# A fixed TensorE order for the first attention, with PSUM banks of its own, in a two-layer diffusion backbone

## The chip, the cores and the metric

The kernel runs on one core of one Trainium2 chip. The metric is the device time of one launch in microseconds (us). A core has a matrix engine (TensorE, PE in the profile), a vector engine (VectorE, DVE), a scalar engine (ScalarE, ACT), GpSimd (POOL) and SyncE (SP), which issues the transfers. Each works through its own instruction list in order, and they wait for each other on counters (semaphores). TensorE writes its results into PSUM, eight banks of 512 fp32 columns on 128 partitions; DVE and ACT read them there.

## The reference

Two DeepNorm layers over 1024 latent tokens and 256 context tokens, width 1024, 16 heads of 64. The change concerns the mixer of the first layer only: windowed attention with a sink, rotary embeddings and a SiLU gate.

```python
def mixer_a(u, uc, w_in, w_out, sink, rope, ctx_out):
    q, k, v, g = _split_a(u @ w_in)          # 16 query heads, 4 key/value heads
    ...                                      # rotary embedding on q and k
    def block(bi):                           # blocks of 128 tokens
        ...
        mask = (jnp.abs(qi[:, None] - kj[None, :]) <= A_WINDOW) & (kj >= 0)[None, :] & (kj < S)[None, :]
        s_lat = jnp.einsum('bqkgd,bjkd->bkgqj', qb, kb).astype(jnp.float32) * scale
        s_lat = jnp.where(mask, s_lat, NEG_INF)
        s_ctx = jnp.einsum('bqkgd,bckd->bkgqc', qb, kc).astype(jnp.float32) * scale
        p = jax.nn.softmax(jnp.concatenate([s_lat, s_ctx, s_sink], axis=-1), axis=-1)
        o = jnp.einsum('bkgqj,bjkd->bqkgd', p_lat, vb) + jnp.einsum('bkgqc,bckd->bqkgd', p_ctx, vc)
    ...
    y = (o * jax.nn.silu(g)) @ w_out
    ...                                      # context tokens attend to the context alone
```

The second layer has a neighbourhood attention in this place; its code is not changed.

## The kernel before

The first attention (attention A) works on eight pairs of heads p; within a pair on ten blocks of 128 tokens b (blocks 8 and 9 are the context), within a block on the two heads h. One (p, b, h) is a *sub*, number k from 0 to 159; the two subs of a block are a *unit*. A sub sees four key tiles of 128 (b = 0 and 7), five (b = 1 to 6) or two (b = 8 and 9). Pair p has subs 20p to 20p + 19.

The steps of a sub k, by engine:
- scores S(k), in `qkA` on TensorE: the query in two halves of precision (l = 0 and 1) against the keys, four matmuls into one tile of two PSUM banks (`S_A`)
- `sm_first`: mask and minimum on DVE (L318), exp on ACT (L325); `sm_second`: reciprocal on DVE (L329), product on POOL (L330)
- transposes T(k), in `sm_transpose` on TensorE (L337): one per key tile, into another tile of two banks (`T_A`); then ACT copies them rounded (the cast, L341, `pth_A`), and DVE subtracts that copy from them (L343, `ptl_A`): the probabilities as a high and a low part. Both parts hold a whole unit and have two buffers
- values of a unit, in `pvA_fn` on TensorE (L734): first with the high part, then with the low part, into one bank for two blocks (`pvA`); behind every odd block the two halves of this bank are added into `otmp` (copy on ACT L743, add on DVE L744) and multiplied by the gate on POOL (L747). After block 9 a pair's result is written out (L751)

PSUM is one pool for the whole kernel: the tag "big" has two slots of two banks, which scores and transposes take in turn, and the tag "one" has four slots of one bank for projections and values.

`att_steps` writes the order of the pieces: row k holds T(k), S(k + 3) and half a unit's values, the high part two rows after the unit's second sub and the low part one row later. `merge` mixes into a pair's rows the projections that fill TensorE, those of the gate of pair p and of the queries of pair p + 1: pieces of 8 × 3 matmuls for each of three chunks (512, 512 and 256 tokens), three matmuls to a piece (L208 to L210: high weight by high and low token parts, low weight by high part). It takes the next fill piece while fill is behind its even share of the cost. The instructions then go to a list scheduler, which sets each engine's order by priorities (`lift`) and readiness, so the built order is not quite the order of the code.

## Time and profile before

| | |
|---|---|
| time, median of 3 runs | 1444.14 us (1442.26 to 1444.5) |
| profiled execution | 1443.36 us, its span 1441.6 us |
| PE busy | 1392.6 us, 97% |
| DVE, ACT, POOL busy | 987.3, 733.6, 630.8 us |
| first attention, first scores to the end of pair 6 | about 98 to 544 us |

The span is the time from the first to the last instruction of the core. The prediction shows the rows it uses of four views: the busy line, windows by stage, the waits of an engine and the timeline. In the timeline a row is the start, the duration, the engine, the line, the operation, output and inputs by their names in the program (numbers left out) and the count of like instructions. A matmul's duration includes its way through the array, so the cost of one on a busy TensorE is the distance to the start of the next.

### The profile page before, as it was taken

Reading aid. Unit: us, or ns where it says so; the run is one execution under the profiler, and the core shown is the slowest. Engines: PE = TensorE matmul, PEld = TensorE weight load, DVE = VectorE, ACT = ScalarE, POOL = GpSimd, SP = SyncE. Lnnn points to the kernel's source line nnn. Section 1 sums busy time; section 2 is a strip of 40 time slices with the busy share of each in tenths; the row PEclk is TensorE's granted clock in tenths of the full one; section 3 lists DMA queues with packets and bytes.
Section 4 is the critical chain, followed back from the end, with each engine's and each line's share of the span. In section 5 each row is a group of like instructions: output and inputs, shape, how many; then the busy total and the mean of one; then the engine's idle time right before and its main releaser. Section 6 shows DMA issues by size and latency. Waiting matters only on the chain. (4 is left out here: it accounts for less than half of the span.)

```text
span 1441.6 us, 25151 instructions
## 1 busy us (share of the span) xinstructions
PE 1392.6 (97%) x8816; PEld 1215.4 (84%) x8816; DVE 987.3 (68%) x2216; ACT 733.6 (51%) x1561; POOL 630.8 (44%) x779
## 2 busy tenths in 40 slices
PE   9999999999999999999999999999999999998995
PEld 5887888888888888788898899888988899887775
DVE  4658888878888789566433765555565565667698
ACT  4336776677676778333222545544454444557310
POOL 0326766666666657233211333333233323336664
PEclk9999999999999999999999999999999999999998
DMA  9472114123122114433287565564555565384353
GB/s 367 171 234 81 53 59 132 46 78 97 66 78 63 56 61 128 128 132 132 74 256 217 160 192 159 140 166 145 170 150 156 144 179 146 103 208 145 115 133 93
DMA packets 117229, 195.05 MB, mean 135 GB/s; under 512 B 9328, under 2 KB 57840, under 8 KB 117104
## 3 DMA queue, kind: packets, MB, share of 16 engines
q1 hardware_dynamic: 117104, 193.45, 44.5%
q8 instruction: 70, 1.15, 0.3%
q14 instruction: 55, 0.45, 0.1%
HBM read 141.51 MB, written 51.90 MB: 134 GB/s over the span
## 5 line engine op out<-in xcount | busy, mean ns | idle before, releaser
L330 POOL TENSOR_SCALAR s_B<-s_B,rs_B 128x640 f32<-128x640 f32 (+1 forms) x128 | 101.9, 797 | 292.0 <-DVE rs_B L329 250.9
L208 PE MATMUL pj<-uBh,wh 128*128 128x512 f32 (+1 forms) x448 | 175.9, 393 | 0.0
L209 PE MATMUL pj<-uBl,wh 128*128 128x512 f32 (+1 forms) x448 | 170.2, 380 | 0.0
L210 PE MATMUL pj<-uBh,wl 128*128 128x512 f32 (+1 forms) x448 | 170.0, 379 | 0.0
L325 ACT ACTIVATE s_B<-s_B,m_B 128x640 f32<-128x640 f32 (+1 forms) x128 | 102.9, 804 | 127.9 <-DVE m_B L318 127.7
L325 ACT ACTIVATE s_A<-s_A,m_A 128x641 f32<-128x641 f32 (+2 forms) x160 | 119.5, 747 | 88.5 <-DVE m_A L318 73.5
L164 POOL TENSOR_TENSOR wl<-wr,wh 128x512 fp32r<-128x512 f32 x64 | 87.7, 1371 | 157.8 <-ACT wh L162 135.4
L330 POOL TENSOR_SCALAR s_A<-s_A,rs_A 128x640 f32<-128x640 f32 (+2 forms) x160 | 127.1, 794 | 58.5 <-DVE rs_A L329 56.3
L318 DVE CUSTOM_DVE_ANT_0 s_A<-S_A,msk,nsk 128x640 f32<-128x640 f32 (+2 forms) x160 | 123.6, 774 | 34.0 <-PE S_A L706 17.7
L343 DVE TENSOR_TENSOR pt_B<-T_B,pt_B 128x640 fp32r<-128x640 f32 (+1 forms) x128 | 101.0, 789 | 63.4 <-ACT pt_B L341 62.9
L208 PE MATMUL pj<-uAh,wh 128*128 128x512 f32 (+1 forms) x384 | 139.9, 364 | 0.0
L209 PE MATMUL pj<-uAl,wh 128*128 128x512 f32 (+1 forms) x384 | 137.6, 358 | 0.0
L210 PE MATMUL pj<-uAh,wl 128*128 128x512 f32 (+1 forms) x384 | 137.3, 357 | 0.0
L343 DVE TENSOR_TENSOR ptl_A<-T_A,pth_A 128x640 fp32r<-128x640 f32 (+2 forms) x160 | 114.0, 713 | 15.3 <-PE pvA L734 7.1
L337 PE MATMUL T_A<-ident,s_A 128*128 128x128 f32 x672 | 101.0, 275 | 12.1 <-DVE m_A L318 8.6
L337 PEld LDWEIGHTS T_A<-ident,s_A 128*128 128x128 f32 x672 | 77.2, 140 | 40.2 <-issue 16.6
L341 ACT CAST pt_B<-T_B 128x640 fp32r<-128x640 f32 (+1 forms) x128 | 84.4, 659 | 47.8 <-PE T_B L337 47.4
L318 DVE CUSTOM_DVE_ANT_0 s_B<-S_B,bias 128x640 f32<-128x640 f32 (+1 forms) x128 | 100.5, 785 | 10.6 <-PE S_B L1037 9.6
L341 ACT CAST pth_A<-T_A 128x640 fp32r<-128x640 f32 (+2 forms) x160 | 96.5, 603 | 16.7 <-PE T_A L337 14.0
L210 PEld LDWEIGHTS pj<-uBh,wl 128*128 128x128 f32 x448 | 84.3, 188 | 16.7
L337 PE MATMUL T_B<-ident,s_B 128*128 128x128 f32 x608 | 88.3, 274 | 6.0 <-POOL gB L1078 2.3
L209 PEld LDWEIGHTS pj<-uBl,wh 128*128 128x128 f32 x448 | 84.7, 189 | 9.1
(219 smaller groups left out, 3885.3 us busy)
## 6 DMA issues: line engine op xcount, KB each, us to landing
kB<-kdB SPq DMA_DIRECT2D x64, 320.0 KB, 5.3
gw<-in_wadaT SPq DMA_DIRECT2D x48, 256.0 KB, 2.8
vdB<-st SPq DMA_DIRECT2D x20, 512.0 KB, 3.4
vB<-vdB SPq DMA_DIRECT2D x16, 640.0 KB, 4.8
wada<-in_wadaC SPq DMA_DIRECT2D x16, 512.0 KB, 9.7
kdB<-st SPq DMA_DIRECT2D x16, 512.0 KB, 2.9
qdB<-st SPq DMA_DIRECT2D x16, 512.0 KB, 3.5
qB<-qdB SPq DMA_DIRECT2D x32, 256.0 KB, 4.6
```

The source lines that it names most:

```text
L164: e.tensor_tensor(lo, r, f32(hi), ALU.subtract)
L208: mm(pt[:, :n], hi[:, sl], rh, start=kt == 0, stop=False)
L209: mm(pt[:, :n], hi[:, sl], rl, start=False, stop=False)
L210: mm(pt[:, :n], lo[:, sl], rh, start=False, stop=kt == KT - 1)
L318: nc.vector.tensor_tensor_reduce(outp, sc, in1, scale, init if init is not None else 3e38, ALU.add, ALU.min, accum_out=s.m)
L325: nc.scalar.activation(s.t[:, :n], s.t[:, :n], AF.Exp, bias=s.m, scale=-1.0, accum_out=s.sum)
L330: nc.gpsimd.tensor_scalar(s.t[:, : s.w], s.t[:, : s.w], s.rs, 1.0, ALU.mult, ALU.mult)
L337: nc.tensor.transpose(tp[:, k * P : (k + 1) * P], s.t[:, src * P : (src + 1) * P], ident)
L341: nc.scalar.copy(pt.hi[:, :n, hl, :], tv)
L343: nc.vector.tensor_tensor(pt.lo[:, :n, hl, :], tv, f32(pt.hi[:, :n, hl, :]), ALU.subtract)
```

## The change

Five things, all of attention A:
- PSUM is opened anew for each stage. In attention A it holds one tile of three banks for all transposes (`T_A`, allocated once: h = 0 uses its left end, h = 1 its right end, where five tiles meet in the middle bank, which is transposed last), one slot of two banks for scores, two slots for projections and one for values. Behind the first block of the output stage it is opened again with the old slots.
- For pairs 0 to 6 all matmuls and transposes are pinned: TensorE keeps the order of the code.
- `merge` takes fill at an even rate, and at most one fill piece with 512 columns between two steps.
- An even block's values go both halves together, in the row where the low half stood; odd blocks stay. In pairs 2, 4 and 6 the first three S pieces stand one step later.
- The copies of a value bank both come before the adds, at a priority of 60.

```diff
--- before.py
+++ after.py
@@ -34,6 +34,7 @@
 
 AHEAD_A, LIFT_A = 3, 80
 AHEAD_B, LIFT_B = 3, 40
+LIFT_PV = 60
 BARE_B = 108
 
 GATED_LAST = 1 << 20
@@ -82,7 +83,16 @@
 
 def build(tc, i, out):
     nc = tc.nc
-    mm = nc.tensor.matmul
+    pinned = []
+
+    def pin(ins):
+
+        if pinned:
+            tc.keep_in_program_order(ins)
+
+    def mm(*a, **kw):
+        pin(nc.tensor.matmul(*a, **kw))
+
     dma = nc.sync.dma_start
     es = ExitStack()
 
@@ -92,13 +102,29 @@
         return p, st
 
     dr = es.enter_context(tc.tile_pool(name="dr", bufs=1, space=DRAM))
-    ps = es.enter_context(tc.tile_pool(name="ps", bufs=1, space=PSUM))
-
-    def psbig(name):
-        return ps.tile([P, 1024], F32, tag="big", bufs=2, name=name)
-
-    def psone(name):
-        return ps.tile([P, 512], F32, tag="one", bufs=4, name=name)
+
+    class Banks:
+
+
+        def open(self, name, att=False):
+            self.st = ExitStack()
+            self.ps = self.st.enter_context(tc.tile_pool(name=name, bufs=1, space=PSUM, reuse_waits="tile"))
+            self.att = att
+            if att:
+
+                self.t3 = self.ps.tile([P, 1536], F32, tag="t3", bufs=1, name="T_A")
+
+        def big(self, name):
+            return self.ps.tile([P, 1024], F32, tag="big", bufs=1 if self.att else 2, name=name)
+
+        def one(self, name):
+            if self.att:
+                return self.ps.tile([P, 512], F32, tag="pv" if name[:2] == "pv" else "pj", bufs=1 if name[:2] == "pv" else 2, name=name)
+            return self.ps.tile([P, 512], F32, tag="one", bufs=4, name=name)
+
+    banks = Banks()
+    banks.open("ps0")
+    psbig, psone = banks.big, banks.one
 
     cp = es.enter_context(tc.tile_pool(name="cp", bufs=1, side="left"))
     ident = cp.tile([P, P], F32, name="ident")
@@ -282,20 +308,24 @@
 
         return evac
 
-    def merge(att, fill, lead=0.0):
+    def merge(att, fill, lead=0.0, burst=1e9):
+
 
         ta = sum(a[0] for a in att) or 1.0
         tf = sum(f[0] for f in fill)
         ia = jf = 0
-        ca = cf = 0.0
+        ca = cf = run = 0.0
         while ia < len(att) or jf < len(fill):
             need = att[ia][2] if ia < len(att) and len(att[ia]) > 2 else 0
-            if jf < len(fill) and (ia == len(att) or jf < need or cf - lead <= ca * (tf - lead) / ta):
+            if jf < len(fill) and (ia == len(att) or jf < need or (run < burst and cf - lead <= ca * (tf - lead) / ta)):
                 cf += fill[jf][0]
+                run += fill[jf][0]
                 fill[jf][1]()
                 jf += 1
             else:
                 ca += att[ia][0]
+                if att[ia][0]:
+                    run = 0.0
                 att[ia][1]()
                 ia += 1
 
@@ -332,9 +362,18 @@
     def sm_transpose(s, order, pt, hl, name):
 
         n = len(order)
-        tp = psbig(f"T_{name}")
-        for k, src in enumerate(order):
-            nc.tensor.transpose(tp[:, k * P : (k + 1) * P], s.t[:, src * P : (src + 1) * P], ident)
+        ks = list(range(n))
+        if name[0] == "B":
+            tp = psbig(f"T_{name}")
+        elif hl == 0:
+            tp = banks.t3[:, : n * P]
+        else:
+
+            tp = banks.t3[:, 1536 - n * P :]
+            ks = ks[1:] + ks[:1]
+        for k in ks:
+            src = order[k]
+            pin(nc.tensor.transpose(tp[:, k * P : (k + 1) * P], s.t[:, src * P : (src + 1) * P], ident))
         tv = tp[:, : n * P].rearrange("p (k q) -> p k q", k=n)
         a = name[0] == "A"
         with lift(20 if a else 0):
@@ -644,6 +683,8 @@
     merge([], vproj_pieces(-1, uA, v_evac(pp, vdA), 2))
     pp_st.close()
     pq, pq_st = pool("attA", "right")
+    banks.st.close()
+    banks.open("psA", True)
 
 
     qA, gA, kA, vA = {}, {}, {}, {}
@@ -738,10 +779,12 @@
         if b % 2 == 1:
             tmp = px.tile([P, 2, P], F32, tag="otmp", bufs=1, name="otmp")
             pv = pvA[p].rearrange("p (b h q) -> p b h q", b=2, h=2)
-            for h in range(2):
-                hs = slice(h * 64, h * 64 + 64)
-                nc.scalar.copy(tmp[hs], pv[64:128, :, h, :])
-                nc.vector.tensor_tensor(tmp[hs], pv[0:64, :, h, :], tmp[hs], ALU.add)
+            halves_ = [(h, slice(h * 64, h * 64 + 64)) for h in range(2)]
+            with lift(LIFT_PV):
+                for h, hs in halves_:
+                    nc.scalar.copy(tmp[hs], pv[64:128, :, h, :])
+                for h, hs in halves_:
+                    nc.vector.tensor_tensor(tmp[hs], pv[0:64, :, h, :], tmp[hs], ALU.add)
             tok = slice((b - 1) * P, (b + 1) * P)
             g = gA[p][:, tok]
             nc.gpsimd.tensor_tensor(g, tmp.rearrange("p b q -> p (b q)"), g, ALU.mult)
@@ -776,14 +819,23 @@
             def v_second(k=k):
                 pv(k - 3, 1)
 
+            def v_both(k=k):
+                pv(k - 3, 0)
+                pv(k - 3, 1)
+
             if -1 <= k < n:
                 row.append((costs[0] if k >= 0 else 0.0, t_piece, 0))
             if k + ahead < n:
                 row.append((costs[1], s_piece, 0))
+
             if split and 0 <= k - 2 < n and last_of_unit(k - 2):
-                row.append((costs[2] / 2, v_first, 0))
+                if subs[k - 2][1] % 2:
+                    row.append((costs[2] / 2, v_first, 0))
             elif split and k - 3 >= 0 and last_of_unit(k - 3):
-                row.append((costs[2] / 2, v_second, need(k - 3, k + ahead)))
+                if subs[k - 3][1] % 2:
+                    row.append((costs[2] / 2, v_second, need(k - 3, k + ahead)))
+                else:
+                    row.append((costs[2], v_both, need(k - 3, k + ahead)))
             elif not split and k - 2 >= 0 and last_of_unit(k - 2):
                 row.append((costs[2], v_piece, need(k - 2, k + ahead)))
             seq.append(row)
@@ -808,8 +860,19 @@
     v_loadA(0)
     merge([], qprojA(0))
     px, px_st = pool("attA2", "right")
+    pinned.append(True)
     for p in range(8):
-        att = [x for row in rowsA[p * 20 : (p + 1) * 20] for x in row]
+        rows_p = [list(row) for row in rowsA[p * 20 : (p + 1) * 20]]
+        if p == 7:
+
+            pinned.clear()
+        elif p % 2 == 0 and p:
+
+            s = [rows_p[n].pop(1) for n in range(3)]
+            rows_p[1].append(s[0])
+            rows_p[2].insert(1, s[1])
+            rows_p[2].append(s[2])
+        att = [x for row in rows_p for x in row]
         if p % 2 == 0 and p:
             k_load(p // 2, 1)
         if p % 2 == 1 and p < 7:
@@ -821,7 +884,7 @@
                 att.insert(3 + g * (n // SEG[p] + 1), dots.pop(0))
             if not dots:
                 att.append((0.0, dots_end, 0))
-            merge(att, gprojA(p) + qprojA(p + 1), lead=0.0)
+            merge(att, gprojA(p) + qprojA(p + 1), lead=1000.0, burst=600.0)
         else:
 
             att += [x for row in rowsA[8 * 20 :] for x in row]
@@ -917,6 +980,9 @@
         if b < 8:
             dma(zdd[b * P : (b + 1) * P, :], z)
         pend = (b, z)
+        if b == 0:
+            banks.st.close()
+            banks.open("psB")
 
     def k_evac(dst, pl):
         def evac(pt, t0, n):
@@ -1240,6 +1306,7 @@
         for sl in parts:
             nc.vector.scalar_tensor_tensor(z[:, sl], z[:, sl], rs[:, 1:2], vecs[3][:, sl], ALU.mult, ALU.add)
             dma(grid_rows(out, b)[:, :, sl], z[:, sl])
+    banks.st.close()
     ob_st.close()
     ub_st.close()
     wp_st.close()
```

Three places show the order that is built; in the names, the number behind S_A, s_A, ptl_A and pth_A is the sub or the unit's first sub, pvA1_0 the values of pair 1 from block 0 on, pj14_1 the projection of weight column 14 for chunk 1, uAh and uAl the token parts, wh and wl the weight parts.

First place, TensorE between T(23) and T(24) in pair 1. Before (T(23) stands three rows above the first):

```order
L208 MATMUL pj14_1_2032<-uAh1_106,wh15_1512 128x512
L209 MATMUL pj14_1_2032<-uAl1_109,wh15_1512 128x512
L705 MATMUL S_A26_2111<-kA0_0_975,qA2_1646 128x384
L706 MATMUL S_A26_2111<-kA0_0_975,qA2_1646 128x256
L705 MATMUL S_A26_2111<-kA0_1_978,qA2_1646 128x384
L706 MATMUL S_A26_2111<-kA0_1_978,qA2_1646 128x256
L210 MATMUL pj14_1_2032<-uAh1_106,wl15_1513 128x512
L734 MATMUL pvA1_0_2129<-pth_A20_1987,vA0_981 128x256 x4
L208 MATMUL pj14_1_2032<-uAh1_106,wh15_1512 128x512
L209 MATMUL pj14_1_2032<-uAl1_109,wh15_1512 128x512
L210 MATMUL pj14_1_2032<-uAh1_106,wl15_1513 128x512
L337 MATMUL T_A24_2141<-ident_63,s_A24_2041 128x128 x5
```

After (matmuls and transposes now go through one wrapper each, L94 and L376):

```order
L376 MATMUL T_A_979<-ident_63,s_A23_1989 128x128 x5
L94 MATMUL S_A26_2089<-kA0_0_980,qA2_1627 128x384
L94 MATMUL S_A26_2089<-kA0_0_980,qA2_1627 128x256
L94 MATMUL S_A26_2089<-kA0_1_983,qA2_1627 128x384
L94 MATMUL S_A26_2089<-kA0_1_983,qA2_1627 128x256
L94 MATMUL pj14_1_2001<-uAh1_106,wh15_1502 128x512
L94 MATMUL pj14_1_2001<-uAl1_109,wh15_1502 128x512
L94 MATMUL pj14_1_2001<-uAh1_106,wl15_1503 128x512
L376 MATMUL T_A_979<-ident_63,s_A24_2027 128x128 x5
```

Between the two groups of transposes stood scores, three pieces of three and four value matmuls; now there are the scores and one piece. The first transpose of a group waits for two counters, one of POOL (the product of its own sub) and one of DVE. Before, DVE's count is that of the step that empties the slot: for 130 groups of the attention the mask step of the sub two on (for T(25) that of sub 27), for 19, T(24) among them, the subtraction of the sub just before. Now it is the subtraction of the sub just before for every group.

DVE at the same place, before:

```order
L343 TENSOR_TENSOR ptl_A22_2056<-T_A22_2057,pth_A22_2055 128x5x128
L329 RECIPROCAL rs_A25_2076<-sum_A25_2075 128x1
L744 TENSOR_TENSOR otmp_2085<-pvA0_8_1979,otmp_2085 64x256
L343 TENSOR_TENSOR ptl_A22_2056<-T_A23_2094,pth_A22_2055 128x5x128
L318 ISA s_A26_2116,m_A26_2117<-S_A26_2111,msk_141,nsk_142 128x640
```

After:

```order
L382 TENSOR_TENSOR ptl_A22_2045<-T_A_979,pth_A22_2044 128x5x128
L359 RECIPROCAL rs_A25_2061<-sum_A25_2060 128x1
L787 TENSOR_TENSOR otmp_2070<-pvA0_8_1996,otmp_2070 64x256 x2
L348 ISA s_A26_2094,m_A26_2095<-S_A26_2089,msk_141,nsk_142 128x640
L348 ISA m_A26_2095 128x1
L382 TENSOR_TENSOR ptl_A22_2045<-T_A_979,pth_A22_2044 128x5x128
```

The mask step of sub 26 stood behind the second subtraction of unit 22; now it stands ahead of it.

Second place, TensorE ahead of T(27). Before:

```order
L734 MATMUL pvA1_0_2129<-ptl_A22_2056,vA0_981 128x256 x5
L208 MATMUL pj14_2_2173<-uAh2_107,wh15_1512 128x256
L209 MATMUL pj14_2_2173<-uAl2_110,wh15_1512 128x256
L210 MATMUL pj14_2_2173<-uAh2_107,wl15_1513 128x256
L208 MATMUL pj16_0_2281<-uAh0_105,wh16_1869 128x512
L209 MATMUL pj16_0_2281<-uAl0_108,wh16_1869 128x512
L210 MATMUL pj16_0_2281<-uAh0_105,wl16_1870 128x512
L337 MATMUL T_A27_2287<-ident_63,s_A27_2154 128x128 x5
```

After:

```order
L94 MATMUL pj14_2_2151<-uAh2_107,wh15_1502 128x256
L94 MATMUL pj14_2_2151<-uAl2_110,wh15_1502 128x256
L94 MATMUL pj14_2_2151<-uAh2_107,wl15_1503 128x256
L94 MATMUL pj16_0_2248<-uAh0_105,wh16_1857 128x512
L94 MATMUL pj16_0_2248<-uAl0_108,wh16_1857 128x512
L94 MATMUL pj16_0_2248<-uAh0_105,wl16_1858 128x512
L94 MATMUL pvA1_0_2142<-ptl_A22_2045,vA0_986 128x256 x5
L376 MATMUL T_A_979<-ident_63,s_A27_2129 128x128 x5
```

The low half of unit 22 had two pieces behind it ahead of T(27); now it stands directly ahead of it.

Third place, the start of attention A on TensorE. Before (the rows end a run of projections):

```order
L208 MATMUL pj10_0_1115<-uAh0_105,wh11_991 128x512
L209 MATMUL pj10_0_1115<-uAl0_108,wh11_991 128x512
L705 MATMUL S_A0_1119<-kA0_0_975,qA0_1030 128x256
L706 MATMUL S_A0_1119<-kA0_0_975,qA0_1030 128x256
L705 MATMUL S_A1_1131<-kA0_0_975,qA1_1031 128x256
L706 MATMUL S_A1_1131<-kA0_0_975,qA1_1031 128x256
L210 MATMUL pj10_0_1115<-uAh0_105,wl11_992 128x512
```

After:

```order
L94 MATMUL pj10_0_1120<-uAh0_105,wh10_990 128x512
L94 MATMUL pj10_0_1120<-uAl0_108,wh10_990 128x512
L94 MATMUL pj10_0_1120<-uAh0_105,wl10_991 128x512
L94 MATMUL S_A0_1124<-kA0_0_980,qA0_1035 128x256 x2
L94 MATMUL S_A0_1124<-kA0_1_983,qA0_1035 128x256 x2
L94 MATMUL pj10_0_1120<-uAh0_105,wh10_990 128x512
```

The scores of the first sub with the second key half (`kA0_1`) stood 19 rows behind those with the first; now they follow at once, behind a single fill piece.

## The prediction

> **What bounds the kernel now.** I read the page's busy line and the clock first, then the kernel's stages one by one: the first attention is the only place that the change reorders.
>
> ```profile
> span 1441.6 us, 25151 instructions
> PE 1392.6 (97%) x8816; PEld 1215.4 (84%) x8816; DVE 987.3 (68%) x2216; ACT 733.6 (51%) x1561; POOL 630.8 (44%) x779
> ```
>
> TensorE is busy 97% of the span. Next, the windows of that attention (columns: stretch, length, busy us of PE, PE's weight loads, DVE, ACT and POOL with counts, granted clock, DMA share, GB/s), and two of the issues on SP that close a head pair.
>
> ```profile
> 98.00:179.00 81.00, 75.40 (x476) 65.07 (x475) 64.96 (x158) 54.58 (x125) 52.12 (x75) 1.00 0.31 90
> 179.00:240.00 61.00, 59.78 (x391) 52.26 (x390) 50.07 (x122) 42.92 (x98) 41.31 (x61) 1.00 0.31 92
> 484.00:544.00 60.00, 57.65 (x381) 50.85 (x380) 50.70 (x128) 43.88 (x98) 37.27 (x55) 1.00 0.20 69
> ...
> 179.04 0.33 SPq L751 DMA_DIRECT2D ogd<-gA  x1
> 543.98 0.33 SPq L751 DMA_DIRECT2D ogd<-gA  x1
> ```
>
> Six pairs take 543.98 − 179.04 = 364.9 us, 60.8 us each. The clock is 1.00 throughout. PE idles a few us in a pair; the waits of PE from 98 to 544 us (who waits, for whom, us in total, times, longest) say for what:
>
> ```profile
> PE T_A L337 <- DVE m_A L318: 6.9, 10, 1.6
> PE S_A L705 <- DVE ptl_A L343: 5.1, 7, 1.2
> PE S_A L706 <- DVE ptl_A L343: 1.8, 6, 0.3
> PE T_A L337 <- POOL gw L619: 1.3, 1, 1.3
> PE T_A L337 <- DVE rs_A L329: 0.5, 1, 0.5
> PE T_A L337 <- POOL s_A L323: 0.4, 1, 0.4
> ```
>
> Together 16.0 us. Transposes (T) and scores (S) share two slots: T(k+1) mostly goes where S(k+3) was, so it waits for the mask step that empties it (m_A), and S(k+4) waits for the subtraction that empties T(k) (ptl). That is all the present order can give back: 16.0 of 446 us.
>
> **What a step costs.** One undisturbed stretch of the timeline (start, duration, engine, line, operation, count, idle before):
>
> ```profile
> 187.42 0.37 ACT L743 COPY otmp<-pvA 64x256 f32<-64x256 f32 x1
> 187.82 0.41 DVE L744 TENSOR_TENSOR otmp<-pvA,otmp 64x256 f32<-64x256 f32 x1 [0.23 <-ACT otmp L743]
> ...
> 190.34 0.74 PE L337 MATMUL T_A<-ident,s_A 128*128 128x128 f32 x5
> ...
> 191.76 0.67 ACT L341 CAST pth_A<-T_A 128x640 fp32r<-128x640 f32 x1
> ...
> 192.38 0.76 PE L734 MATMUL pvA<-ptl_A,vA 128*128 128x256 f32 x5
> 192.98 0.39 PE L208 MATMUL pj<-uAh,wh 128*128 128x512 f32 x1
> 193.21 0.39 PE L209 MATMUL pj<-uAl,wh 128*128 128x512 f32 x1
> 193.25 0.82 DVE L343 TENSOR_TENSOR ptl_A<-T_A,pth_A 128x640 fp32r<-128x640 f32 x1 [0.35 <-PE pvA L734]
> 193.66 0.71 PE L337 MATMUL T_A<-ident,s_A 128*128 128x128 f32 x5
> 194.13 0.44 PE L705 MATMUL S_A<-kA,qA 128*128 128x384 f32 x1
> 194.41 0.70 ACT L341 CAST pth_A<-T_A 128x640 fp32r<-128x640 f32 x1 [0.48 <-PE T_A L337]
> 194.81 0.39 PE L208 MATMUL pj<-uAh,wh 128*128 128x512 f32 x1
> 195.12 0.89 DVE L318 CUSTOM_DVE_ANT_0 s_A<-S_A,msk,nsk 128x640 f32<-128x640 f32 x1 [0.98 <-POOL s_A L330]
> 195.50 0.76 PE L734 MATMUL pvA<-pth_A,vA 128*128 128x256 f32 x5
> 196.09 0.39 PE L208 MATMUL pj<-uAh,wh 128*128 128x512 f32 x1
> 196.78 0.71 PE L337 MATMUL T_A<-ident,s_A 128*128 128x128 f32 x5
> 197.24 0.42 PE L705 MATMUL S_A<-kA,qA 128*128 128x384 f32 x1
> 197.58 0.69 ACT L341 CAST pth_A<-T_A 128x640 fp32r<-128x640 f32 x1 [0.52 <-PE T_A L337]
> 199.89 0.71 PE L337 MATMUL T_A<-ident,s_A 128*128 128x128 f32 x5
> ...
> 232.13 0.69 DVE L343 TENSOR_TENSOR ptl_A<-T_A,pth_A 128x512 fp32r<-128x512 f32 x1
> ...
> 302.85 0.82 DVE L343 TENSOR_TENSOR ptl_A<-T_A,pth_A 128x640 fp32r<-128x640 f32 x1
> 303.72 0.44 PE L705 MATMUL S_A<-kA,qA 128*128 128x384 f32 x1 [0.53 <-DVE ptl_A L343]
> ```
>
> PE's cost of a piece is the distance between starts: a 512-wide projection matmul 0.23 (192.98 to 193.21), a piece of three 0.69 (196.09 to 196.78), values of five tiles 0.59 (195.50 to 196.09), five transposes 0.47 (193.66 to 194.13), scores of one sub 0.68 behind transposes (194.13 to 194.81) and 0.59 elsewhere. Two whole rows, 193.66 to 196.78 and 196.78 to 199.89, take 3.1 us each with no gap: PE is full here.
>
> The helpers' chain from one transpose: cast begins 0.80 after it (196.78 to 197.58) and lasts 0.70, ptl lasts 0.82, and a PE instruction that waits for ptl starts 0.05 after its end (302.85 + 0.82 to 303.72). Sum: **2.37 us from T(k) to the end of the wait for ptl(k)**. A ptl that must wait for the low-half values before it, whose buffer it overwrites, starts 0.87 after their first matmul (192.38 to 193.25): 0.87 + 0.82 + 0.05 = 1.74. A cast that must wait for the high-half values: 0.87 + 0.70 + 0.82 + 0.05 = 2.44.
>
> **The change, part by part.** No matmul is added or removed: PE's own work of a pair, all pieces at the costs above, stays 56.5 us. What moves is who waits for whom.
>
> *The ring.* All transposes of attention A now write one tile of three banks, allocated once. The built program lets the first transpose of every T(k+1) wait for the DVE count that ptl(k) reaches, in units of two, four and five tiles alike. So T, cast, ptl, T is a ring of 2.37 us (five tiles; for four tiles about 2.0, an estimate from a ptl of 0.69 at 232.13 and a cast and transposes shorter in proportion), and it costs nothing only where PE has as much work between T(k) and T(k+1). Before, that distance was covered by the slots in nearly every row. After, the order is fixed and at most one piece of 512 stands between two steps of the attention. I laid PE's new order of the second pair out at the costs above and took the missing cover, row by row:
> - T(23) to T(24): transposes 0.47, scores 0.67, one piece 0.69, in all 1.83 against 2.37: 0.55 short. T(31) and T(35) lack 0.67 each. Sum 1.9.
> - Rows with both value halves behind an even T(k) (k = 20, 24, 28, 32): the cast of T(k) waits for the high half, 2.44 from its start, less what follows it: 0.60 to 0.71 each, 2.6 in all.
> - Rows with the low half behind an even T(k) (k = 22, 26, 30, 34): ptl(k) waits for it. Ahead of T(27) these values come last: 1.74 − 0.59 = 1.15 short. The four lack 2.8.
>
> That is 7.3 us in a pair. Counted the same way, pairs 0 to 6 have 6.0, 5 times 7.3 and 6.6: **49.0 us**. Pair 7 is not pinned and lacks under 1 us; I leave it out.
>
> *What goes.* The 16.0 us of waits for shared slots: T has banks of its own, and S(k+1) waits for the mask step of S(k) alone, which has a row's time. I subtract all of it; if late masks keep some, the forecast grows by up to 16.0.
>
> *Order of the helpers.* DVE works in order. The mask step of S(26), 0.89 long, now stands ahead of the second subtraction of unit 22, which is ptl(23). S(26) ends 0.47 + 0.68 = 1.15 after T(23), its mask step at 2.04, ptl at 2.86, and T(24) comes at 2.91 instead of 2.37: 0.54 more. ACT can do the same with an exp ahead of a cast: the cast at 191.76 began 1.42 after its transposes at 190.34, 0.62 later than the chain needs; before, that cost nothing. Ends: 0, if all such rows have slack, and 32, from a walk by hand through the second pair with every helper in its listed place (up to 70 us a pair: 9.2 above now, times 7 is 64, less the net 33 = 49 − 16 counted above). I take **16**, the middle, which is also both delays twice in a pair: 2 × 1.16 × 7.
>
> *The start.* Rows of PE, and the loads of the keys on SP, with the time from issue to landing:
>
> ```profile
> 95.05 0.40 PE L208 MATMUL pj<-uAh,wh 128*128 128x512 f32 x1
> ...
> 98.25 0.28 PE L705 MATMUL S_A<-kA,qA 128*128 128x256 f32 x1
> ...
> 102.16 0.28 PE L705 MATMUL S_A<-kA,qA 128*128 128x256 f32 x1
> ...
> 91.84 2.57 SPq L679 DMA_DIRECT2D kA<-kdA  x4
> ...
> DMA to landing us min/median/max: 3.7/4.9/7.9
> ```
>
> Before, 14 projection matmuls run from 95.05 and the halves of the first scores at 98.25 and 102.16. After, one piece of three (0.69) is followed by both halves of S(0), pinned, and whatever is behind them waits too. The last of the four loads is issued by 91.84 + 2.57 = 94.4 and lands between 98.1 (3.7) and 99.7 (if the first took the longest, 7.9); until then PE has the 0.69 and the first half, 0.36. Idle: 98.1 − 95.05 − 1.05 = 2.0 to 3.6, and up to 1.5 behind it, where only one piece fills each step. Ends 2 and 5; I take **4.0**, since landings of the slow end go with four loads issued at once.
>
> *Small edits.* The sums of the value halves (copies first, then adds, at a higher priority) matter where the one pv bank must be free for the next values: a unit pair's values come four subs apart, over 4 us, and the two copies of 0.37 and two adds of 0.41 (187.42, 187.82) that empty it take 1.6 one after another. Cost nothing; if the cover went, 2 us a pair. The reopening of the banks after the attention can hold the next stage's first tiles: 0 to 3, taken as 0. The scores of even pairs moved one step later stay within the count above. SP issues the same transfers in the same order.
>
> **Sum**, against the profiled execution, 1443.4 (its span 1441.6 and 1.8 around it; the median of the runs is 1444.1): 1443.4 + 49.0 − 16.0 + 16 + 4.0 = 1496.4, so **1496**.
>
> **A rule against the trace.** The clock was 1.00 in every stretch above, with single waits of up to 1.6 us in them. The Trainium skill, page "TensorE: Matmul & The Clock Gate", section "A second HAM failure mode: psum-queue depth-cycling", says that frequent small idles between groups of matmuls, from cycling through PSUM banks, can make the clock fall back again and again. The trace does not agree as yet: 26 such waits left it at 1.00. By that rule the ring would cost more than its gaps; I add nothing, and a granted clock of 0.9 in the new windows would prove me wrong by about 40 us.
>
> **The rivals.**
> - *The ends are independent (faster).* T(k+1) uses the other end of the tile, so the data would only ask for ptl(k−1). Were that what TensorE waits for, a row more would lie between, 5 us against 2.4, the 49.0 and the 16 vanish: 1443.4 − 16.0 + 4.0 = 1431. It decides from the point where PE's waits between 95 and 544 us stay below 12 us. For it: ends that don't overlap. Against: the count that the first transpose waits for. Chance 0.12.
> - *Only the middle bank binds.* Two five-tile subs meet in one bank, and its tile is transposed last. Were only this transpose to wait, each need falls by four transposes, 0.37, and four-tile units drop out: 2.3 short in a pair, 16 in seven; 1443.4 + 16 − 16 + 16 + 4.0 = 1463. Chance 0.07. The Trainium skill, "PSUM — Partial Sum Buffer", section "Terms", forbids two engines in one bank at a time and so asks for no more than this; whether the chip's waits do, no row of before shows.
> - *The waits only change their names.* The new gaps come to what the old ones were less the start, 16 − 4 = 12 us: 1443. That needs three quarters of the 49 to be covered by PE work that my costs leave out and helpers that are never late. The two gapless rows above, in which the costs fit to 0.02, speak against it. Chance 0.04.
> - *Worse than the ring.* The helpers' order at its full 32 and a start of 5: 1443.4 + 49.0 − 16.0 + 32 + 5 = 1513; a clock that drops comes on top. Chance of more than 1518: 0.04.
>
> **How the numbers follow.** The ring as summed, with helpers between 0 and 32 and the start between 2 and 5, gives 1478 to 1513, and 1464 where the shortfalls are a third smaller; with a few us for the banks reopened, 1464 to 1518: chance 0.73. The runs before spread from 1442.3 to 1444.5, so 0.2% (3 us) is about what can be told from no change. Faster 0.12, no change 0.04, slower the rest, 0.84. The range takes in the middle-bank case and no change and leaves out the faster case and the worst: 1442 to 1518.
>
> **What would show it.** Right: transposes that wait for ptl at L382 lead PE's waits, some 45 to 65 us from 95 to 544, in gaps of 0.5 to 1.5; a pair takes 65 to 69 us; S(0) starts its second half near 99.5 after an idle of 2 to 4. Wrong: a pair near 59 with no such waits (independent ends), or waits at one transpose in five (middle bank). Wrong for another reason: a clock below 1.00 in the pairs.

## The result, and the profile after

The changed kernel takes 1541.3 us (median of 4 runs, 1539.0 to 1547.2), against 1444.3 before: a ratio of 1.068, 95% interval 1.066 to 1.071. It is 97 us slower. The way and the place were forecast, the size was not: 1496 with a range up to 1518.

The busy line after:

```profile
span 1539.9 us, 25192 instructions
PE 1406.2 (91%) x8815; PEld 1216.0 (79%) x8816; DVE 993.4 (65%) x2216; ACT 734.8 (48%) x1561; POOL 617.2 (40%) x779
```

The work is the same and the span longer: TensorE falls from 97 to 91%. Its busy time grew by 13.6 us with the same matmuls. One part of that is what runs out ahead of a wait: the row at 344.69 below is busy to 345.09 where the next would have started at 344.92, so this wait costs 0.17 us more than it is listed with. Another part is the clock, which was at half in three stretches up to 210 us (last section). How much each makes was not separated. Two of the issues on SP that close a pair:

```profile
197.48 0.33 SPq L794 DMA_DIRECT2D ogd<-gA  x1
635.57 0.33 SPq L794 DMA_DIRECT2D ogd<-gA  x1
```

And the windows of two pairs (columns as before):

```profile
345.50:419.30 73.80, 60.39 (x384) 51.46 (x384) 50.63 (x124) 44.31 (x101) 38.50 (x58) 1.00 0.27 75
419.30:491.20 71.90, 60.07 (x384) 51.39 (x384) 50.76 (x124) 41.69 (x95) 38.95 (x58) 1.00 0.16 50
```

A pair takes (635.57 − 197.48) / 6 = 73.0 us instead of 60.8. The first pair ends 18.4 us later than before, the seventh 91.6, and the next stage's first transposes 96.2 (697.7 instead of 601.5). The waits of TensorE from 95 to 640 us:

```profile
PE T_A L376 <- DVE ptl_A L382: 64.4, 66, 2.6
PE T_A L376 <- DVE rs_A L359: 19.6, 20, 2.0
PE S_A L94 <- DVE m_A L348: 5.5, 7, 2.8
PE T_A L376 <- POOL s_A L360: 1.9, 4, 0.9
PE T_A L376 <- POOL gA L790: 0.3, 1, 0.3
```

The ring leads, as forecast, and it is longer than its first line. The second line is the ring too: in each of its 20 waits a reciprocal (rs_A), 0.15 us long, stands on DVE directly behind the subtraction, and the profile names the later of the two; but the transposes begin 0.15 us after the subtraction's end, as they do in the 66 waits of the first line. One of the 20:

```profile
212.75 0.82 DVE L382 TENSOR_TENSOR ptl_A<-T_A,pth_A 128x640 fp32r<-128x640 f32 x1
213.50 0.15 DVE L359 RECIPROCAL rs_A<-sum_A 128x1 f32<-128x1 f32 x1
...
213.72 0.74 PE L376 MATMUL T_A<-ident,s_A 128*128 128x128 f32 x5 [1.01 <-DVE rs_A L359]
```

So 86 waits and 84.0 of the 91.7 us are the ring's. One turn of it, T(63) to T(64), from TensorE, ACT and DVE:

```profile
343.07 0.74 PE L376 MATMUL T_A<-ident,s_A 128*128 128x128 f32 x5 [0.40 <-DVE ptl_A L382]
343.56 0.83 PE L94 MATMUL S_A<-kA,qA 128*128 128x384 f32 x4
344.69 0.40 PE L94 MATMUL pj<-uAh,wl 128*128 128x512 f32 x1
346.49 0.74 PE L376 MATMUL T_A<-ident,s_A 128*128 128x128 f32 x5 [1.39 <-DVE ptl_A L382]
...
343.85 0.69 ACT L380 CAST pth_A<-T_A 128x640 fp32r<-128x640 f32 x1
...
344.71 0.88 DVE L348 CUSTOM_DVE_ANT_0 s_A<-S_A,msk,nsk 128x640 f32<-128x640 f32 x1
345.52 0.82 DVE L382 TENSOR_TENSOR ptl_A<-T_A,pth_A 128x640 fp32r<-128x640 f32 x1
```

This is the predicted row, with the cast 0.78 after the transposes, done at 344.54; then DVE is in the mask of S(66) to 345.5, subtracts to 346.34, and T(64) follows. One turn 3.42 us. Over the 72 five-tile subs of pairs 1 to 6 the subtraction ends 3.57 us after the transposes began (2.37 was the bare chain), and T follows T at 3.87. In the kernel before, the same mean is 3.54, with T behind T at 3.17: the helpers were as late there, and the two shared slots hid it.

And there is a wait that the prediction does not have, ahead of the attention, at its first projection:

```profile
86.04 0.42 DVE L293 SCALAR_TENSOR_TENSOR st<-pv-1_2_798,st 128x256 fp32r<-128x256 f32 x1 [0.45 <-ACT st L292]
...
86.61 0.77 PE L94 MATMUL pj<-uAh,wh 128*128 128x512 f32 x1 [5.07 <-DVE st L293]
87.17 0.63 PE L94 MATMUL pj<-uAl,wh 128*128 128x512 f32 x1
...
89.73 0.43 PE L94 MATMUL pj<-uAl,wh 128*128 128x512 f32 x1
```

The reopened PSUM gives it a bank from which DVE still reads projected values (`pv-1_2`, those of blocks 4 and 5) until 86.46; before, a free slot was taken at 81.28 without a wait.

### The profile page after: what moved, and what is told of

The parts are those of the page before. It is cut to its first block, busy times and chain, and to the rows that moved or that the text cites. A ratio compares the mean times of both kernels' runs of the same rounds, so it can differ in the third digit from the quotient of the medians.

```text
span 1539.9 us, 25192 instructions
## 1 busy us (share of the span) xinstructions
PE 1406.2 (91%) x8815; PEld 1216.0 (79%) x8816; DVE 993.4 (65%) x2216; ACT 734.8 (48%) x1561; POOL 617.2 (40%) x779
## 5 line engine op out<-in xcount | busy, mean ns | idle before, releaser
L376 PE MATMUL T_A<-ident,s_A 128*128 128x128 f32 x672 | 102.5, 277 | 87.3 <-DVE ptl_A L382 65.4
L94 PE MATMUL pj<-uBh,wh 128*128 128x512 f32 (+1 forms) x448 | 175.9, 393 | 0.0
L376 PEld LDWEIGHTS T_A<-ident,s_A 128*128 128x128 f32 x672 | 73.8, 140 | 125.4 <-issue 38.0
L94 PE MATMUL pj<-uBl,wh 128*128 128x512 f32 (+1 forms) x448 | 170.3, 380 | 0.0
L94 PE MATMUL pj<-uBh,wl 128*128 128x512 f32 (+1 forms) x448 | 170.0, 380 | 0.0
L360 POOL TENSOR_SCALAR s_A<-s_A,rs_A 128x640 f32<-128x640 f32 (+2 forms) x160 | 121.1, 757 | 120.6 <-DVE rs_A L359 116.8
L94 PE MATMUL pj<-uAh,wh 128*128 128x512 f32 (+1 forms) x384 | 146.0, 380 | 5.2 <-DVE st L293 5.1
L94 PE MATMUL pj<-uAh,wl 128*128 128x512 f32 (+1 forms) x384 | 137.9, 359 | 0.0
L94 PE MATMUL pj<-uAl,wh 128*128 128x512 f32 (+1 forms) x384 | 137.8, 359 | 0.0
L94 PE MATMUL S_A<-kA,qA 128*128 128x384 f32 (+1 forms) x576 | 112.9, 313 | 10.1 <-DVE m_A L348 10.1
L94 PEld LDWEIGHTS S_A<-kA,qA 128*128 128x128 f32 x576 | 90.0, 191 | 25.5 <-DVE m_A L348 16.4
L348 DVE CUSTOM_DVE_ANT_0 s_B<-S_B,bias 128x640 f32<-128x640 f32 (+1 forms) x128 | 100.3, 784 | 11.5 <-PE S_B L94 10.2
L94 PE MATMUL yA<-woAh,og 128*128 128x512 f32 x320 | 103.4, 395 | 0.0
```

The source lines that it names most:

```text
L94: pin(nc.tensor.matmul(*a, **kw))
L348: nc.vector.tensor_tensor_reduce(outp, sc, in1, scale, init if init is not None else 3e38, ALU.add, ALU.min, accum_out=s.m)
L360: nc.gpsimd.tensor_scalar(s.t[:, : s.w], s.t[:, : s.w], s.rs, 1.0, ALU.mult, ALU.mult)
L376: pin(nc.tensor.transpose(tp[:, k * P : (k + 1) * P], s.t[:, src * P : (src + 1) * P], ident))
```

## The experiments

All ratios are to the kernel before, with 95% intervals; "a pair" is its mean over pairs 1 to 6 as above. "Free" or "freed" means that the list scheduler orders TensorE's instructions when the program is built, and "pinned" that it keeps the order of the code; on the chip TensorE works through a given list either way.

**Undo one part at a time.** Four kernels, each the changed one with a single edit. The ring cut to the fifth key tile (`x_three`):

```diff
-                self.t3 = self.ps.tile([P, 1536], F32, tag="t3", bufs=1, name="T_A")
+                self.tx = [self.ps.tile([P, 512], F32, tag=f"t{x}", bufs=1, name=f"T_A{x}") for x in "012"]
...
+            parts = [(0, m, banks.tx[hl][:, : m * P])]
+            if n == 5:
+                parts.append((4, 1, banks.tx[2][:, hl * P : hl * P + P]))
```

> The changed kernel with the one transpose tile of three banks cut into three tiles of a bank each: four key tiles of h = 0, four of h = 1, and the fifth of both, whose cast and subtraction come as instructions of their own, first. T(k+1) then waits only for ptl(k-1) and, at its last transpose, for the small subtraction of the fifth tile of sub k. Adds one cast and one subtraction to every five-tile sub. Theory ring (T(k+1) waits for ptl(k), the wait of 64 us): most of the 92 us of waits go, 1455 to 1480. Rival fixed order (what costs is that TensorE may no longer pass late scores and late helpers): the waits come back at other names, 1510 to 1540.

Measured 1497.3 us, 1.037 (1.035 to 1.039), a pair 66.3 us. Of the 97 us 44 came back, and the time lies between the two expectations: 53 us stay. TensorE's largest waits from 95 to 640 us:

```profile
PE T_A L376 <- DVE ptl_A L384: 38.1, 55, 2.2
PE S_A L94 <- DVE m_A L348: 12.8, 13, 2.8
```

All 55 waits of the first line are at a fifth transpose and end with the small subtraction that reads the shared third tile. So a smaller ring is left, and this run does not show what the order would cost with none.

Priorities of the helpers (`x_lift`):

```diff
-        with lift(20 if a else 0):
+        with lift(90 if a else 0):
...
-        with lift(60 if a else 0):
+        with lift(100 if a else 0):
```

> The changed kernel with the cast at priority 90 and the subtraction at 100 instead of 20 and 60, above the masks and exps (80). Theory helper order (inside the ring, casts begin 1.5 us after the transposes instead of 0.8, since exps and gate evacuations stand ahead of them on ACT, and masks ahead of subtractions on DVE): the ring falls from 3.6 toward 2.6 us a five-tile sub, 1480 to 1505, cast lag near 0.9. Rival value order (the casts are late since the high-part values that free their buffer are): 1530 to 1545 with the same lag.

Measured 1536.0, 1.065 (1.062 to 1.067), with the casts 1.46 us behind the transposes (1.52 in the changed kernel). Priority is not it; the rival as stated is not shown either, since something else may put them late.

Free scheduling (`u_pin`):

```diff
-    pinned.append(True)
```

> The changed kernel without pinning: the scheduler may move TensorE's instructions in all pairs, all else as changed. Theory ring: the wait of T(k+1) for ptl(k) stays, but the scheduler can put fill into it, so a part returns, 1470 to 1500. Rival fixed order alone: everything returns, at or below 1444. Rival neither: 1535 to 1545.

Measured 1471.2, 1.019 (1.017 to 1.021), a pair 63.0. Freed, TensorE hardly waits for the ring at all:

```profile
PE S_A L94 <- DVE m_A L348: 14.2, 20, 2.1
PE T_A L376 <- DVE ptl_A L382: 2.4, 8, 0.6
```

The scheduler puts other work where the ring's gaps would be. Undoing this one edit gives 70 us back, more than any other. The longest waits left are those for the single slot for scores, but that slot is not what the remaining 27 us are: with the banks of before, freed (`u_bankpin` below), the time is only 2.6 us shorter.

Values of even blocks halved again (`u_vals`):

```diff
-                if subs[k - 2][1] % 2:
-                    row.append((costs[2] / 2, v_first, 0))
+                row.append((costs[2] / 2, v_first, 0))
...
-                if subs[k - 3][1] % 2:
-                    row.append((costs[2] / 2, v_second, need(k - 3, k + ahead)))
-                else:
-                    row.append((costs[2], v_both, need(k - 3, k + ahead)))
+                row.append((costs[2] / 2, v_second, need(k - 3, k + ahead)))
```

> The changed kernel with the values of even blocks halved over two rows as before, all else as changed. In the changed kernel the longest steps, 5.0 to 5.8 us, are those four of a pair behind which both value halves stand (about 2 us each over the work in them, 8 us a pair, 56 in seven). Theory values (the cast waits for the late high half): 1490 to 1510. Rival ring (the chain is as long in other rows): 1530 to 1545.

Measured 1516.2, 1.050 (1.048 to 1.053), a pair 69.9; casts now 0.97 us behind the transposes. It falls between the two expectations: 25 us came back, not 31 to 51. The longest steps went, and the subtractions were later by themselves, 0.79 us behind their casts (0.54 in the changed kernel), nearly the length of a mask.

**Banks, order and pins apart.** The banks of before, all else changed, pinned (`u_bank`) and free (`u_bankpin`); and the kernel before, only pinned (`o_pin`). Of the expectations of the first two one phrase is wrong: PSUM was still closed and opened again in both.

```diff
-        if name[0] == "B":
+        if name[0] == "B" or not banks.att:
...
-    banks.open("psA", True)
+    banks.open("psA")
```

> The changed kernel with the banks of before in the first attention (two slots that scores and transposes take in turn, four for projections and values, PSUM not reopened), all else as changed: pinned, even fill, both value halves together. Theory banks (the ring through the one transpose tile, the one slot for scores and the reopening are what costs): the 44 us that three tiles gave back and more, 1465 to 1485. Rival fixed order (any bank layout waits as long when TensorE may not pass a late step): 1505 to 1540.

> The changed kernel with the banks of before and without pinning: what is left of the change is the even fill, the values of even blocks together, the sums of the value banks at their higher priority, and the scores moved one step. Theory banks and pin carry everything: within 0.5% of the kernel before, 1437 to 1451. Rival: the order of the values costs by itself, 1460 to 1470 (25 us came back when it alone was undone).

> The kernel before with one thing added: TensorE's instructions of pairs 0 to 6 pinned to the order of the code. Theory fixed order: the scheduler's order is worth as much here, 1480 to 1515 (70 us came back when the changed kernel was freed). Rival ring (pinning costs only with the ring, since shared slots wait for steps that are long done): 1444 to 1460.

`u_bank` took 1500.3 us, 1.039 (1.038 to 1.041), a pair 66.6, between its two theories; `u_bankpin` 1468.6, 1.017 (1.015 to 1.018), a pair 61.4; `o_pin` 1479.3, 1.024 (1.022 to 1.026), a pair 65.3. So the new banks cost 41 us where TensorE is pinned (1541.3 − 1500.3) and 2.6 where it is free (1471.2 − 1468.6): the ring costs little without the pins. And pins cost 35 us by themselves, in the order of before, with no ring. The largest waits of `o_pin`:

```profile
PE T_A L345 <- DVE m_A L326: 17.2, 31, 1.5
PE S_A L92 <- DMA kA<-kdA: 12.5, 4, 3.8
PE S_A L92 <- DVE ptl_A L351: 8.5, 12, 1.0
```

The old waits, 15.5 us of them in the same stretch of the kernel before and none for keys, have grown to 38 us, 12.5 of them for keys that have not landed. In the order that the scheduler builds, other work stands ahead of such steps, as at the start of the attention (the third place under "The change"). What these runs compare is the code's order with the scheduler's; TensorE pinned to the scheduler's own order was not tried.

**The other sequence of banks** (`x_order`: the projections' banks first, the transposes' behind them).

> The changed kernel with the same banks laid out in another sequence: the two of the projections first, where the keys' projection was read out long before, instead of behind transposes and scores, where TensorE waited 5.1 us at 81.5 us for the readout of the context values. Theory reopening (that wait and the slower clock behind it, matmuls of 0.43 instead of 0.23 us up to 89.7, are lost for good): 5.1 + 1.6 = 6.7 us less, 1533 to 1536. Rival (the time is waited for again at the first scores, whose keys land near 100 us): 1538 to 1543.

Measured 1550.3, 1.073 (1.072 to 1.075), slower than the changed kernel by 9 us. The 5.07 us wait fell to 1.5, but the first pair ends only 1.0 us earlier (196.44), near what the rival had: at the start there is now a wait of 1.8 us for keys, and one of 1.7 for a mask. (The expectation's "context values" are the values of blocks 4 and 5, as shown above.) And at the other end the reopened banks give a wait that the changed kernel has not:

```profile
692.84 0.80 PE L94 MATMUL yA<-woAh,og 128*128 128x512 f32 x1 [8.30 <-DVE z L977]
```

**Scores behind the values** (`x_late`, with the values halved; `x_latethree` also with three tiles). Both also leave out the change's moving of three S pieces in pairs 2, 4 and 6, which their expectations do not say.

```diff
-            if k + ahead < n:
+            if k + ahead < n and not (split and k >= 0):
                 row.append((costs[1], s_piece, 0))
...
+            if k + ahead < n and split and k >= 0:
+                row.append((costs[1], s_piece, 0))
             seq.append(row)
```

> The changed kernel with two edits: the values of all blocks halved over two rows as before (which alone gave 25 us back, 1516), and in each row the scores last, behind fill and values, instead of right behind the transposes. The mask step of sub k+3 is then ready only after the subtraction of sub k, so DVE does the subtraction first. Theory helper order (in the run with halved values the subtraction still began 0.80 us after its cast, as long as a mask lasts, and a mask that is ready first goes first whatever its priority): subtraction 0.1 to 0.3 after the cast, the ring near 2.6 us instead of 3.3, a pair 64 to 66 us instead of 69.9, 1475 to 1492. Rival: the delay comes from elsewhere, 1505 to 1520.

> The same two edits and the three transpose tiles of a bank each, pinned. Theory: ring and helper order were the two losses, and what is left is a fixed order that nothing late breaks: a pair at 61 to 63 us, 1455 to 1470. Rival fixed order (a loss of some 5 us a pair that goes with pinning whatever the tiles): a pair at 65 to 67, 1485 to 1500.

`x_late` took 1503.9, 1.041 (1.039 to 1.042), a pair 67.8. The mechanism is as stated: subtractions now begin 0.30 us behind their casts instead of 0.79, and the waits listed for them fall from 51.3 to 28.8 us. The gain is 12 us where 24 to 41 were expected; other waits come up:

```profile
PE T_A L376 <- DVE ptl_A L382: 28.8, 28, 2.9
PE pvA L94 <- DVE otmp L787: 9.9, 29, 0.8
PE S_A L94 <- DMA kA<-kdA: 8.9, 3, 3.2
```

One is the single bank for values, whose sums the prediction had put at nothing. `x_latethree` took 1482.9, 1.026 (1.024 to 1.028), a pair 64.6: closer to the fixed order's rival, 38 us above the kernel before with ring, long casts and late subtractions all treated. Its waits for subtractions are down to 7.2 us; the largest now are 10.2 for the bank of the values and 8.3 for keys.

**Single parts added to the kernel before.** Even fill (`o_fill`), values together (`o_vals`), and PSUM closed and opened at the two places with its old slots (`o_reopen`).

```diff
-            merge(att, gprojA(p) + qprojA(p + 1), lead=0.0)
+            merge(att, gprojA(p) + qprojA(p + 1), lead=1000.0, burst=600.0)
```

> The kernel before with only the even fill (at most one piece of 512 columns between two steps), unpinned. Theory: the rows stay covered since the scheduler moves fill, only the start waits 5 to 6 us for the keys: 1446 to 1453. Rival: the even fill carries most of the 24 us that the order costs without banks and pins, 1460 to 1470.

> The kernel before with only the values of even blocks together, unpinned. Theory: the scheduler covers a later cast with fill, 1443 to 1449. Rival: the values carry most of the 24 us, 1455 to 1468.

> The kernel before with one thing added: its PSUM pool closed and opened again at the two places of the change, ahead of the first attention's projections and behind the first block of the output stage, with the same tags and slots. (The two runs with the banks of before, u_bank and u_bankpin, still reopened PSUM, against what their expectations say.) Theory reopening (a new tile in a reopened bank waits for the last readout there, and the scheduler counts on a bank it does not get): the start 5 to 8 us later and a wait of 7 to 9 us at the first output matmuls, 1456 to 1468. Rival (the even fill, the values and the priority of the sums together cost it): 1443 to 1448.

`o_fill` 1442.6, 0.999 (0.998 to 1.000): no start wait, a pair 60.4, and at most a gain of 0.2%; it is the only version that came out below the kernel before. `o_vals` 1445.4, 1.001 (0.999 to 1.002). `o_reopen` 1458.0, 1.009 (1.008 to 1.011): 13.6 us for an edit that changes no slot. (The edit, like the change, also gives the PSUM pool the option `reuse_waits="tile"`; the next two runs have it without reopening.) Its waits show both ends, the output matmuls and the keys at the start:

```profile
PE yA L427 <- DVE z L919: 8.2, 1, 8.2
PE T_A L344 <- DVE m_A L325: 6.9, 12, 1.5
PE S_A L714 <- DMA kA<-kdA: 5.3, 2, 3.3
```

**The same order, never reopened.** `u_bankpin` and `u_bank` without the two edits of the PSUM pool: `y_order` (free) and `y_pin` (pinned).

```diff
-    banks.st.close()
-    banks.open("psA")
...
-        if b == 0:
-            banks.st.close()
-            banks.open("psB")
```

> The run with the banks of before and without pins (1468.6), its PSUM pool never reopened: even fill, values together, sums at their priority, scores one step later, and nothing else of the change. Theory reopening: 1441 to 1447, as the even fill and the values alone. Rival (the rest of the order costs): 1460 to 1470.

> The same with pins (1500.3 with PSUM reopened), never reopened. Theory: reopening takes about 20 us off, and what is left is what pinning costs in either order (the kernel before, pinned, took 1479.3): 1475 to 1484. Rival (reopening costs less where TensorE's order is fixed, since nothing moves into its place): 1492 to 1502.

`y_order` took 1453.8, 1.006 (1.005 to 1.008), a pair 61.4, between its two theories; `y_pin` 1490.8, 1.032 (1.031 to 1.033), a pair 66.4, near its rival. Reopening costs 14.8 us free and 9.5 pinned; the order without banks and pins keeps 9.4, in the priority of the sums, the scores moved, the pool's option, or the parts together. Which of them was not tried.

## Why the prediction was right in sign and wrong in size

The loss can be split in two ways. The first is by the changed kernel's own trace. Its profiled span grew by 98.3 us, where the sum had 53.0: 5.5 up to T(0) (110.83 against 105.32), 86.1 from there to the end of the seventh pair, where the sum had 49 (49.0 + 16 − 16.0), 4.6 to the next stage's first transposes and 2.1 behind them. Of the 86.1, 72 are idle time of TensorE and 14 are added busy time, for which the sum had nothing.

The second is a ladder of runs with one step to each edit: before 1444.4; the order alone 1453.8 (+9.4); pinned 1490.8 (+37.0); PSUM reopened 1500.3 (+9.5); one tile for all transposes, one slot for scores and the split of the other banks 1541.3 (+41.0). These steps depend on their sequence, as the free runs show: the last is 2.6 without pins.

- *The ring and the helpers' order, 49.0 + 16.* The mechanism stands, and this term was made too small: 84.0 us of waits in 86 turns, against 65, or 81 with the helpers at their upper end. Two readings failed. The chain of 2.37 us was put together from undisturbed rows; over all five-tile subs of pairs 1 to 6 it was 3.57 us, and 3.54 already before, which the trace of before could have told. And a transpose begins 0.15 us behind the end of the subtraction (346.34 to 346.49), where 0.05 was taken from a row of scores: some 9 us over 86 turns, by estimate. In the ladder the step measures only 41: as the step before it shows, much of this time would be lost with the old slots as well.
- *What goes, −16.0.* The waits for shared slots did nearly go: from T(0) to the end of the seventh pair 5.0 us are left that are not the ring's, 2.8 of them at the slot for scores. The step that failed is the one behind this term, that the rest of the order runs at TensorE's costs, so that without the ring the kernel would take 1431 (the sum of the first rival). The code's order, pinned, with the old slots and no ring, takes 1490.8, +37.0 over the same parts free, and +35 in the order of before; the waits for shared slots grow there instead of going. I had counted cover only for the one wait that the change adds, not for the waits that the scheduler's order had been covering.
- *The start, 4.0, and the reopening, taken as 0.* Reopening costs 9.5 pinned and 13.6 alone, at both ends. The end of the attention, 0 to 3 in the text, has waits of 8 us in four other runs. In the changed kernel the start is 5.5 us late, near the 4.0, but this is luck: no wait for keys is listed there, and S(0) runs in one go at 102.68. What it has is the wait for a bank, 5.07 us, that I did not look for, and one of 2.75 for a mask at the single slot for scores.
- *Small edits, 0.* The even fill, and the values of even blocks together, each added alone and free, cost nothing, as forecast. The order as a whole costs 9.4 free. In the changed kernel, pinned and with the ring, the values together cost 25 (`u_vals`).

By the ladder, 65 to 41, −16 to +37, 4 to 9.5 and 0 to 9.4: −24 + 53 + 5.5 + 9.4 = +44, the miss of 97 against 53. By the trace, 19 for the ring, 5 for other waits, 14 for busy time, 1.5 at the start and 6.7 behind the seventh pair make 46, against a miss of 45 in the profiled span. The two agree in what the sum lacked: it priced waits that can be counted in one row and took the rest of a pinned order as free.

Of the rivals, independent ends are excluded by the ring's waits. The middle bank alone is what `x_three` comes near to: that rival's sum was 1463, and the run took 1497. "Worse than the ring" came true, partly for the reason it names, helpers at their upper end.

What would show it right did so in kind and not in size: a pair of 73 rather than 65 to 69, 92 us of waits rather than 45 to 65, single ones up to 2.6 rather than 1.5. The sign of another cause, a clock below 1.00 in the pairs, came once, for 3.4 us in pair 1. What the cast waits for is shown only in part: values together make it late (1.52, and 0.97 without), priorities do not.

## What to carry to other kernels

An order taken over from the code can cost more than the waits that one counts in it: a late step behind which a scheduler would not have put the rest becomes a stop for the whole engine, and short waits in a profile that a scheduler has ordered are not a measure of the slack. Before an order is pinned, pin the old one alone and look what that costs. And before a chain of helpers is made a ring, take its length as the mean over all its rows, not from the best one: here 3.54 us against 2.37. A pool that is closed and opened again with the very same slots can cost 1% at its two ends, since the first tiles inherit the last readers of their banks; look for the readout that ends last there, at both ends.

## What the runs showed of the hardware

The granted clock fell to half behind idles that are shorter than I had thought of: these are windows of the changed kernel behind waits of 2.60 us (before 204.72) and 2.75 us (before 106.76).

```profile
204.70:206.00 1.30, 1.28 (x11) 1.30 (x12) 0.00 (x0) 0.50 (x1) 1.30 (x3) 0.94 0.00 0
206.00:208.00 2.00, 2.00 (x10) 2.00 (x10) 1.27 (x2) 0.78 (x2) 1.24 (x2) 0.50 0.00 0
...
106.76:110.10 3.34, 3.34 (x12) 2.95 (x13) 2.44 (x6) 1.95 (x5) 1.48 (x4) 0.51 0.64 185
```

It stayed at half for 3.41 us each time (86.38 to 89.79, 106.86 to 110.27 and 205.85 to 209.26 by the trace's record of the clock), and a matmul of 512 columns came every 0.43 us instead of 0.23 (six such distances from the row at 87.17 to that at 89.73, both shown above, behind 5.07 us). Behind waits of 2.01 to 2.07 us of this kernel it stayed at 1.00, and so it did in the pairs' windows above, whose waits are shorter. But the length alone does not decide. In `u_vals` three waits of 2.05 us (before 207.14, 346.92 and 487.26) were followed by such a stretch, and a fourth of 2.05 us (before 559.28) was not; in `x_late` even a wait of 3.10 us (before 377.01) was not. The three stretches above begin 6 and 29 times 3.413 us apart, and the five of `u_vals` from 84 to 490 us begin 7, 29, 41 and 41 times that apart, so that where a wait falls in the grid may decide; no run tests that.

The Trainium skill, "TensorE: Matmul & The Clock Gate", section "HAM oscillation — how this bites in real kernels", puts the limit at gaps of about 3.4 us; here 2.05 could suffice. The Trainium skill's section "A second HAM failure mode: psum-queue depth-cycling" on the same page, which the prediction weighed, has small frequent idles do this: of the 98 waits of the attention only the two of 2.6 us and more were followed by a lower clock in the trace's record, and the two windows of whole pairs shown above hold 1.00.
